# An encoder layer on one NeuronCore: more pairs of seven products in the up projection, and edits around its beginning and around the down projection

## The chip, the core and the metric

The kernel runs on one core of a Trainium2 chip. A core has TensorE (PE in the profile; PEld is its weight load), VectorE (DVE), ScalarE (ACT), GpSimd (POOL) and SyncE (SP); SBUF is the working memory of 128 partitions, PSUM the eight accumulator banks of TensorE, and DRAM the memory off the core. The metric is the device time of one execution in microseconds (us); less is better.

## The reference

One layer of an encoder: 256 tokens, width 2048, all in float32. The first half has two attention branches, a gate for each and an output projection. Its second half, which the change touches, is a squared-ReLU MLP between two RMS norms with a residual sum:

```python
y = jnp.einsum('bsd,de->bse', mixed, w_out[l])
x = x + rms_norm(y, norm_mix_post[l])
h = rms_norm(x, norm_mlp_pre[l])
u = jnp.square(jax.nn.relu(jnp.einsum('bsd,df->bsf', h, w_up[l])))
x = x + rms_norm(jnp.einsum('bsf,fd->bsd', u, w_down[l]), norm_mlp_post[l])
```

`w_up` is 2048 x 8192 and `w_down` 8192 x 2048: the up and the down projection each read 64 MB of weights and take half of the matmul work between them.

## The kernel before, in words

**Products in three matmuls.** Each float32 operand is split into a high and a low part (ACT casts the high part, DVE subtracts it to get the low part), and each product is three matmuls: high times high, high times low, low times high (`Products.add`, L642 to 653). All their records stand at L649.

**Pairs by eight or by seven.** Weights come in tiles of 256 rows by 1024 columns, called a pair here (two blocks of 128 rows); `pair_weights` (L602) loads one on SP's queue and splits it. With the 256 tokens as two blocks of 128, a pair is a 2 x 2 by 2 x 2 block product. `eight` forms it in the plain way: for each of four output pieces two products, 24 matmuls. `seven` uses Strassen's scheme in Winograd's form: seven products, 21 matmuls. For that the weights' sums are formed too (L614 to 616, L626, L627 on DVE and ACT; names with `t`, `eh`, `el`) and the activations' sums (`sums_of`, L714).

**Banks.** The plain pieces accumulate in products 1, 2, 3 and 7, in the four banks of the pool `mm`. Products 0, 4, 5 and 6, which only pairs of seven use, lie in the four banks of the pool `ms` from the first pair of seven of a group to its last, when `combine` (L673) adds them up on DVE. The transposes through PSUM (`bank(name)`) use `ms` too.

**Up projection (L1025 to 1057).** Eight groups of 1024 columns, each `wide_group` (L682) over eight pairs. Group 0 runs all pairs by eight; groups 1 to 7 run `UPS`, pairs 3 and 5 by seven. The gate groups earlier in the kernel run `MIXED` (L749), pairs 0, 3 and 6 by seven. At each pair a hook (`up_each`) emits side work: in group 0 the rest of the residual rows and their transposes (`residual_parts`, L865; results `h2T`), the squares for the norm (`mlp_squares`) and the sums for the pairs of seven (`h2sum`); in the others the transposes, squares (L1012) and splits of what the group before gave, half a group at pair 1 and half at pair 2 (`u_sets`, L1001, and `act_sets`, L944). These are written to DRAM on POOL's queue (`keeph`, `keepl`).

**Before the up projection.** The last group of the output projection is finished row block by row block; `between` (L896) emits the first two `residual_parts` of rows 0 to 127 between its products. `post_norm` gives the scale `ry` of a row block through a power on POOL (L86 to 89).

**Down projection (L1100 to 1143).** Two halves `g` of 1024 output columns. Each runs blocks of four pairs; the activations come back from DRAM on ACT's queue (`act_again`, L976; names `bh`, `bl`). In most blocks two of the four pairs go by seven, in the first and in the last block of each half one. In the last block `in_order` chains the matmuls in program order; the last pair's four pieces go one by one to DVE and ACT (`down_piece`, L1078), and `finish` (L1087) forms the norm of a row block, adds the residual `x2` and writes the rows out.

**Buffers and order.** SBUF tiles of 4 KB a partition come from a pool of 27 pages; weights have three buffers each for the raw tile, the high and the low part, the sums' parts five. The order of instructions on each engine is fixed ahead by a planner that goes by program order and by a timeline with estimated durations; `issue_after` lets an instruction come behind a given one on its engine. Each engine works its list in that order.

Of the kernel before, what the change touches and what calls it, by code (L numbers as in the profile page):

```python
# [38 lines left out]
def encoder_layer(ctx: ExitStack, tc: tile.TileContext, a, out):  # L39
# [42 lines left out]
    def inv_rms(ss, n, name, r=None):  # L82

        w = ss.shape[1]
        ms_ = small(w, f"{name}_m")
        nc.vector.tensor_scalar(ms_, ss, 1.0 / n, EPS, op0=ALU.mult, op1=ALU.add)  # L86
        if r is None:
            r = small(w, f"{name}_r")
        nc.gpsimd.tensor_tensor(r, ms_, expo[:, :w], op=ALU.pow)
        return r  # L90


    last_load = [None]

# [507 lines left out]
    def pair_weights(view, name, seven, low=None):  # L602


        raw = wp.tile([P, 4, 512], F32, tag="raw", name=f"{name}r")
        last_load[0] = nc.sync.dma_start(raw.rearrange("p (h b) c -> p h (b c)", h=2), view).ins
        h1, l1 = wtile("hi", f"{name}h"), wtile("lo", f"{name}l")
        if not seven:
            nc.scalar.copy(h1, raw)  # L609
            nc.vector.tensor_sub(l1, raw, h1.bitcast(F32))  # L610
# [3 lines left out]
        nc.vector.tensor_add(t[0], raw[:, 1:3], raw[:, 0:1].to_broadcast([P, 2, 512]))  # L614
        nc.vector.tensor_add(t[1][:, 0], t[0][:, 0], raw[:, 2])
        nc.vector.tensor_add(t[1][:, 1], t[1][:, 0], raw[:, 3])
        nc.vector.tensor_sub(l1[:, 1:4], raw[:, 1:4], h1[:, 1:4].bitcast(F32))
        h2, l2 = [], []
        for i in range(2):
            for part, n in ((h2, "eh"), (l2, "el")):  # L620
                shape, n = [P, 2, 512], f"{name}{n}{i}"
                if low and part is l2:
                    part.append(low(shape, F32R, n))
                else:
                    part.append(mid.tile(shape, F32R, tag="e", name=n))
            nc.scalar.copy(h2[i], t[i])  # L626
            nc.vector.tensor_sub(l2[i], t[i], h2[i].bitcast(F32))  # L627
        return h1, l1, h2, l2
# [3 lines left out]
    class Products:  # L632
# [22 lines left out]
        def seven(self, stat, w, last):  # L655
# [3 lines left out]
            self.add(0, stat(0), r, 1, last)  # L659
            self.add(2, stat(6), r, 2)  # L660
            self.add(1, stat(1), r, 3)
            self.add(4, stat(3), t[0], 0, last)
# [19 lines left out]
    def wide_group(name, kinds, view, stat7, stat8, mm_banks, z, piece, each=None, turn=None):  # L682
# [5 lines left out]
        for n, (i, seven) in enumerate(kinds):  # L688
            if each:
                each(n)  # L690
            w = pair_weights(view(i), f"{name}_{i}", seven)
# [203 lines left out]

    def between(i):  # L896
        return residual_parts(0, i - 5)[0] if i in (5, 6) else None
# [27 lines left out]

    def first_up(n):
# [12 lines left out]
    kept = {}  # L939
# [85 lines left out]
    UPS = [(0, 0), (1, 0), (2, 0), (3, 1), (4, 0), (5, 1), (6, 0), (7, 0)]  # L1025
    uz = None
    for g in range(DFF // 1024):
        z = [page([P, 2, 512], F32, f"u{g}{t}") for t in range(2)]

        def up_each(n, g=g, uz=uz):  # L1030
            if not g:
                first_up(n)
                if n == 7:
                    for i in (3, 5):
# [5 lines left out]
            elif n in (1, 2):  # L1040
                u_sets(g * 2 - 3 + n, uz)
# [3 lines left out]
            UPS if g else ALL8,  # L1045
# [9 lines left out]
            turn=None if g else partial(residual_parts, 1, 0),  # L1055
# [31 lines left out]
    def finish(t):  # L1087
# [3 lines left out]
        for c in range(4):  # L1091
# [3 lines left out]
                z, z, rd, x2[t * 2 + c // 2][:, cs], op0=ALU.mult, op1=ALU.add  # L1095
# [5 lines left out]
    for g in range(2):  # L1101
        pr = Products(f"p{g}", (1, 2, 3, 7))
        for bi, b in enumerate(blocks[g]):
            end = bi == len(blocks[g]) - 1
            if bi == 0:
                steps = [(b + 1, 0, 0), (b, 1, 0), (b, 0, 1), (b + 1, 1, 0)]
# [5 lines left out]
            for n, (cg, j, seven) in enumerate(steps):  # L1112
# [9 lines left out]
                if g == 1 and bi == 5 and n == 0:  # L1122
                    gp2 = [page([P, 1024], F32, f"gp2{h}") for h in range(2)]
                    for h in range(2):
# [3 lines left out]
                        )  # L1128
                if g == 1 and bi == 6:
# [69 lines left out]
```

## Time and profile before

| | |
|---|---|
| three runs | 1367.77, 1370.4, 1371.29 us (median 1370.4) |
| profiled execution, its own time | 1367.94 us |
| its span, first to last instruction | 1366.2 us |
| granted TensorE clock, mean | 0.997 |
| busy: PE, PEld, DVE, ACT, POOL | 98%, 82%, 76%, 53%, 2% |
| moved between DRAM and SBUF | 329.57 MB, 241 GB/s |
| up projection, first to last product | about 659 to 1016 us of the span |
| down projection | about 1017 us to the end |

Times in the rows are microseconds from the start of the span. A row of a timeline gives start, length, engine, line, operation, output<-inputs with partitions x elements, and in brackets how long the engine had been idle and what ended it. Durations of neighbouring rows on one engine can overlap, so the price of an operation in a row of them is the distance from start to start.

### The profile page before, as it was taken

The page shows a single profiled execution, that of the slowest core. Times are in us where ns is not written, and L with a number is a line of the kernel's source. Part 1 is how long each engine was busy: PE and PEld are TensorE (multiplying, and loading weights), DVE is VectorE, ACT ScalarE, POOL GpSimd, SP SyncE. Part 2 cuts the span into 40 slices and gives each one's busy share as a digit, 9 for nine tenths or more (in the row PEclk, how much of TensorE's full clock was granted, in tenths as well). Part 3 has the DMA queues.
Part 4 walks back from the last instruction along what each step waited for, and adds up shares of the span by engine and source line. Part 5 has one row for each costly group of instructions (what it writes and reads, how often), then busy time and mean ns, then how long its engine had stood idle before and what let it go on. Part 6 is the DMA issues. An engine that isn't in the chain of part 4 may idle for free.

```text
span 1366.2 us, 16268 instructions
## 1 busy us (share of the span) xinstructions
PE 1340.7 (98%) x6347; PEld 1119.4 (82%) x6347; DVE 1034.7 (76%) x1181; ACT 717.8 (53%) x843; POOL 33.9 (2%) x67
## 2 busy tenths in 40 slices
PE   7999999999999999999999999999999999999996
PEld 6888888888888888888788888888887788888885
DVE  6878866667857886654768887888788888798886
ACT  7455455555644464344465655666555555454542
POOL 0000000000000000000000000000000000000000
PEclk9999999999999999999999999999999999999998
DMA  8675645564556655676367766786697999698891
GB/s 306 201 227 168 202 161 175 166 206 154 185 185 213 218 185 185 204 264 205 134 207 260 259 244 243 258 287 231 249 336 282 386 355 373 239 385 346 340 352 74
DMA packets 115245, 329.57 MB, mean 241 GB/s; under 512 B 17120, under 2 KB 18400, under 8 KB 115168
## 3 DMA queue, kind: packets, MB, share of 16 engines
q1 hardware_dynamic: 96784, 264.03, 56.1%
q10 hardware_dynamic: 12240, 40.91, 7.7%
q0 software_dynamic: 6144, 23.60, 4.3%
q8 instruction: 50, 0.82, 0.2%
q14 instruction: 27, 0.22, 0.0%
HBM read 302.81 MB, written 27.51 MB: 242 GB/s over the span
## 4 chain that ended last, share of the span: by engine, by line
PE 96%; DVE 1%; DMA 1%; issue 0%; ACT 0%; ACTq 0%; SPq 0%; DVEq 0%; POOLq 0%; POOL 0%
PE u L649 25%; PE p L649 23%; PE ga L649 6%; PE gb L649 6%; PE ba L649 3%; PE bb L649 3%; PE qa_p L192 2%; PE ka_p L192 2%; PE qn_p L192 2%; PE kn_p L192 2%; PE y_p L230 2%; PE y_p L231 2%; PE y_p L232 2%; PE qa_p L193 1%; PE qn_p L193 1%; PE kn_p L193 1%
## 5 line engine op out<-in xcount | busy, mean ns | idle before, releaser
L117 DVE TENSOR_TENSOR y_l<-y_w,y_h 128x1024 fp32r<-128x1024 f32 x32 | 37.9, 1222 | 30.9 <-ACT y_h L116 30.9
L116 ACT CAST y_h<-y_w 128x1024 fp32r<-128x1024 f32 x32 | 32.0, 1047 | 40.9 <-PE y_p L232 32.6
L230 PE MATMUL y_p<-y_h,mh 128*128 128x512 f32 x128 | 50.1, 391 | 0.0
L231 PE MATMUL y_p<-y_l,mh 128*128 128x512 f32 x128 | 49.9, 390 | 0.0
L232 PE MATMUL y_p<-y_h,ml 128*128 128x512 f32 x128 | 49.8, 390 | 0.0
L192 PE MATMUL qa_p<-hT,qa_h 128*128 128x512 f32 x128 | 47.1, 413 | 1.2 <-DVE hT L275 1.2
L649 PE MATMUL u<-u_0h,h2T 128*128 128x512 f32 x128 | 44.6, 392 | 2.3 <-DVE ry_m L86 1.1
L192 PE MATMUL qn_p<-hT,qn_h 128*128 128x512 f32 x128 | 45.9, 400 | 0.0
L192 PE MATMUL kn_p<-hT,kn_h 128*128 128x512 f32 x128 | 45.4, 398 | 0.0
L192 PE MATMUL ka_p<-hT,ka_h 128*128 128x512 f32 x128 | 45.0, 398 | 0.0
L649 PE MATMUL u<-u_1h,h2T 128*128 128x512 f32 x128 | 44.6, 396 | 0.0
L649 PE MATMUL u<-u_4h,h2T 128*128 128x512 f32 x128 | 42.1, 390 | 0.0
L649 PE MATMUL u<-u_2h,h2T 128*128 128x512 f32 x128 | 41.8, 397 | 0.0
L649 PE MATMUL u<-u_6h,h2T 128*128 128x512 f32 x128 | 41.8, 389 | 0.0
L649 PE MATMUL u<-u_7h,h2T 128*128 128x512 f32 x128 | 41.0, 389 | 0.0
L193 PE MATMUL qn_p<-hT,qn_l 128*128 128x256 f32 x128 | 35.9, 281 | 0.0
L193 PE MATMUL kn_p<-hT,kn_l 128*128 128x256 f32 x128 | 35.7, 280 | 0.0
L193 PE MATMUL qa_p<-hT,qa_l 128*128 128x256 f32 x128 | 35.2, 285 | 0.0
L193 PE MATMUL ka_p<-hT,ka_l 128*128 128x256 f32 x128 | 35.2, 280 | 0.0
L609 ACT CAST u_1h<-u_1r 128x2048 fp32r<-128x2048 f32 x8 | 15.3, 1913 | 36.1 <-PE u L649 32.6
L649 PEld LDWEIGHTS u<-u_0h,h2T 128*128 128x128 f32 x128 | 23.9, 188 | 8.4 <-DVE ry_m L86 1.6
L192 PEld LDWEIGHTS qa_p<-hT,qa_h 128*128 128x128 f32 x128 | 24.6, 194 | 6.7 <-DVE hT L275 1.6
(1386 smaller groups left out, 4346.8 us busy)
## 6 DMA issues: line engine op xcount, KB each, us to landing
y_w<-in_w_out SPq DMA_DIRECT2D x16, 1024.0 KB, 5.3
bh<-keeph ACTq DMA_DIRECT2D x30, 512.0 KB, 9.2
bl<-keepl ACTq DMA_DIRECT2D x30, 512.0 KB, 11.1
keeph<-ah POOLq DMA_DIRECT2D x18, 512.0 KB, 3.4
keepl<-al POOLq DMA_DIRECT2D x18, 512.0 KB, 7.2
ka_w<-in_w_in SPq DMA_DIRECT2D x8, 1024.0 KB, 5.7
va_w<-in_w_in SPq DMA_DIRECT2D x8, 1024.0 KB, 5.0
qn_w<-in_w_in SPq DMA_DIRECT2D x8, 1024.0 KB, 5.1
```

The lines of the kernel that those rows point to most:

```text
L116: nc.scalar.copy(hi[part], raw[part])
L117: nc.vector.tensor_sub(lo[part], raw[part], hi[part].bitcast(F32))
L192: nc.tensor.matmul(ps[b], hi[:, k % 4, cs], mv, start=(k == 0), stop=False)
L193: nc.tensor.matmul(ps[b][:, :T], lo[:, k % 4, cs], mv[:, :T], start=False, stop=(k == nk - 1))
L230: nc.tensor.matmul(ps[t], sh, hi[:, k % 4], start=(k == 0), stop=False)
L231: nc.tensor.matmul(ps[t], sh, lo[:, k % 4], start=False, stop=False)
L232: nc.tensor.matmul(ps[t], sl, hi[:, k % 4], start=False, stop=(k == nk - 1))
L609: nc.scalar.copy(h1, raw)
L649: ins = nc.tensor.matmul(self.ps[i], st, mv[:, blk], start=i not in self.begun, stop=last and n == 2).ins
```

## The change

In the up projection, groups 1 to 7 run the order `MIXED` and so have three pairs by seven, one of them (pair 0) second in the group; `h2sum` is formed for pairs 0, 3 and 6; both `u_sets` are emitted at pair 1; and `seven` issues its products in the order 2, 1, 0, 4, 6, 5, 3. In group 0, two subtractions of weights (`u_1l` and `u_2l`) get a place on DVE: `u_1l` behind the last DVE instruction (a low half of `h2T`) of the second of the two `residual_parts` in `between`, `u_2l` behind the scaling in the last `inv_rms`, which is that of `post_norm` for rows 128 to 255. After the squares of group 0 the four pages of `x2` are written to DRAM, and they are loaded again as `x3` at the first pair of the last block, on ACT's queue. In the down projection the first block of the first half has no pair by seven, and in the very last block the last two pairs are worked together, piece by piece.

```diff
 def inv_rms:
-        nc.vector.tensor_scalar(ms_, ss, 1.0 / n, EPS, op0=ALU.mult, op1=ALU.add)
+        scaled[0] = nc.vector.tensor_scalar(
+            ms_, ss, 1.0 / n, EPS, op0=ALU.mult, op1=ALU.add
+        ).ins
...
-    def pair_weights(view, name, seven, low=None):
+    def pair_weights(view, name, seven, low=None, after=None):
...
             nc.scalar.copy(h1, raw)
-            nc.vector.tensor_sub(l1, raw, h1.bitcast(F32))
+            with tc.issue_after(after) if after else nullcontext():
+                nc.vector.tensor_sub(l1, raw, h1.bitcast(F32))
...
-            self.add(0, stat(0), r, 1, last)
             self.add(2, stat(6), r, 2)
             self.add(1, stat(1), r, 3)
+            self.add(0, stat(0), r, 1, last)
...
+    tail = []
+
     def between(i):
-        return residual_parts(0, i - 5)[0] if i in (5, 6) else None
+        if i in (5, 6):
+            last, act, vec = residual_parts(0, i - 5)
+            tail.append((act, vec))
+            return last
...
     def first_up(n):
         for t, c in {2: [(1, 1), (0, 2)], 3: [(1, 2), (0, 3)], 4: [(1, 3)]}.get(n, ()):
             residual_parts(t, c)
+        if n == 1:
+            return tail[1][1]
+        if n == 2:
+            return scaled[0]
         if n == 5:
             for t in range(2):
                 mlp_squares(t)
                 mlp_scale(t)
+            for i in range(4):
+                kd = dram.tile([P, 1024], F32, name=f"keepx{i}", tag=f"keepx{i}")
+                nc.gpsimd.dma_start(kd, x2[i])
+                kept["x", i] = kd
...
-    UPS = [(0, 0), (1, 0), (2, 0), (3, 1), (4, 0), (5, 1), (6, 0), (7, 0)]
...
             if not g:
-                first_up(n)
+                after = first_up(n)
                 if n == 7:
-                    for i in (3, 5):
+                    for i in (0, 3, 6):
...
-            elif n in (1, 2):
-                u_sets(g * 2 - 3 + n, uz)
+                return after
+            elif n == 1:
+                for q in (2, 1):
+                    u_sets(g * 2 - q, uz)
...
-            UPS if g else ALL8,
+            MIXED if g else ALL8,
...
             z = zw[c // 2, t][:, c % 2]
             nc.vector.scalar_tensor_tensor(
-                z, z, rd, x2[t * 2 + c // 2][:, cs], op0=ALU.mult, op1=ALU.add
+                z, z, rd, x3[t * 2 + c // 2][:, cs], op0=ALU.mult, op1=ALU.add
             )
...
             if bi == 0:
-                steps = [(b + 1, 0, 0), (b, 1, 0), (b, 0, 1), (b + 1, 1, 0)]
+                steps = [(b + 1, 0, 0), (b, 1, 0), (b, 0, g), (b + 1, 1, 0)]
...
+                if end and g and n == 0:
+                    x3 = [page([P, 1024], F32, f"x3{i}") for i in range(4)]
+                    for i in range(4):
+                        nc.scalar.dma_start(x3[i], kept["x", i])
...
                 last = end and n == 3
+                if g and end and n > 1:
+                    ahead = [*ahead, (cg, j, w)] if last else [(cg, j, w)]
+                    if not last:
+                        continue
+                else:
+                    ahead = [(cg, j, w)]
                 for which in range(4):
-                    pr.eight(partial(dstat8, sets[g, cg], cg, j), w, which, last)
+                    for m, (cc, jj, ww) in enumerate(ahead):
+                        pr.eight(
+                            partial(dstat8, sets[g, cc], cc, jj), ww, which, last and m == len(ahead) - 1
+                        )
```

More of the change, by code (lines that the diff above doesn't have):

```diff
@@ L93, in encoder_layer @@
     last_load = [None]
+    scaled = [None]
     def load(src, k0, nk, c0, cw, name):
@@ L688, in wide_group @@
         for n, (i, seven) in enumerate(kinds):
-            if each:
-                each(n)
-            w = pair_weights(view(i), f"{name}_{i}", seven)
+            after = each(n) if each else None
+            w = pair_weights(view(i), f"{name}_{i}", seven, after=after)
             if seven:
@@ L894, in residual_parts, with turn_rows @@
         return last.ins, act.ins, vec.ins
+    tail = []
     def between(i):
-        return residual_parts(0, i - 5)[0] if i in (5, 6) else None
+        if i in (5, 6):
+            last, act, vec = residual_parts(0, i - 5)
+            tail.append((act, vec))
+            return last
+    def turn_rows():
+        residual_parts(1, 0)
     def mlp_squares(t):
@@ L924, in encoder_layer @@
         )
+    kept = {}
     def first_up(n):
@@ L932, in first_up @@
                 mlp_scale(t)
+            for i in range(4):
+                kd = dram.tile([P, 1024], F32, name=f"keepx{i}", tag=f"keepx{i}")
+                nc.gpsimd.dma_start(kd, x2[i])
+                kept["x", i] = kd
     NG = DFF // 512
     FIRST = (NG - 4, NG - 2)
-    kept = {}
     def seven_of(cg):
@@ L1054, in encoder_layer @@
             each=up_each,
-            turn=None if g else partial(residual_parts, 1, 0),
+            turn=None if g else turn_rows,
         )
```

## The prediction

> **What bounds the kernel now.** I read the page's busy times and the chain of waits first, then busy times by stretch, then each engine's timeline in the stretches that the change touches.
>
> ```profile
> PE 1340.7 (98%) x6347; PEld 1119.4 (82%) x6347; DVE 1034.7 (76%) x1181; ACT 717.8 (53%) x843; POOL 33.9 (2%) x67
> PE 96%; DVE 1%; DMA 1%; issue 0%; ACT 0%; ACTq 0%; SPq 0%; DVEq 0%; POOLq 0%; POOL 0%
> ```
>
> TensorE (PE) is the chain. So there are three ways to win: fewer products, fewer of the few gaps on PE, and a shorter stretch behind its last product. By stretch (start:end, length, then PE, PEld, DVE, ACT, POOL busy, granted clock, DMA share, GB/s):
>
> ```profile
> 440.80:482.30 41.50, 41.50 (x185) 34.37 (x184) 36.26 (x34) 22.08 (x17) 0.00 (x0) 1.00 0.59 203
> 640.00:664.00 24.00, 21.77 (x98) 16.97 (x96) 14.94 (x22) 11.07 (x17) 0.55 (x1) 1.00 0.51 173
> 664.00:711.00 47.00, 46.92 (x219) 39.00 (x220) 30.80 (x59) 30.17 (x54) 1.67 (x3) 1.00 0.52 176
> 843.00:887.00 44.00, 44.00 (x204) 36.47 (x203) 35.85 (x35) 25.99 (x26) 3.22 (x6) 1.00 0.74 257
> 1019.00:1063.00 44.00, 41.53 (x182) 31.75 (x180) 34.39 (x31) 25.92 (x26) 3.19 (x6) 1.00 0.79 299
> 1063.00:1107.00 44.00, 42.89 (x188) 35.19 (x189) 40.87 (x35) 23.45 (x19) 0.00 (x0) 1.00 0.95 364
> ```
>
> The first row is a gate group in the order MIXED (three pairs of seven), the fourth an up group with two: PE has no gap in either. The gaps are 2.2 us where the up projection begins (second row) and 2.5 + 1.1 = 3.6 us where the down projection begins (the last two). The clock is 1.00, so a product saved is worth its full-speed time.
>
> **Price of a product.** From the chain of waits (start, length, what):
>
> ```profile
> 802.80 0.77 PE uT L1009 x7
> 846.91 0.77 PE uT L1009 x7
> 853.30 37.67 PE u L649 x166
> ```
>
> 166 products in 37.67 us are 0.227 us each; one up group lasts 846.91 - 802.80 = 44.1 us. A pair by eight products is 24 matmuls (each product is hi-hi, hi-lo, lo-hi), by seven 21: it saves 3 x 0.227 = 0.68 us. The Trainium skill ("TensorE: Matmul & The Clock Gate", Back-to-back issue gap) gives about 131 ns for a sustained 512-column matmul; by it seven more pairs would save 2.8 us. The rows above disagree at 227 ns, and the measurement decides.
>
> **Part 1, up groups 1 to 7.** Three pairs of seven for two: 7 x 0.68 = **-4.8 us** on PE, if VectorE (DVE) keeps up. Its price for the two kinds of pair, start to start in its timeline:
>
> ```profile
> 842.11 2.29 DVE L610 TENSOR_TENSOR u_1l<-u_1r,u_1h 128x2048 fp32r<-128x2048 f32 x1
> 844.31 2.28 DVE L610 TENSOR_TENSOR u_2l<-u_2r,u_2h 128x2048 fp32r<-128x2048 f32 x1
> 859.43 1.22 DVE L614 TENSOR_TENSOR u_3t<-u_3r 128x1024 f32<-128x1024 f32 x1
> 860.57 1.75 DVE L617 TENSOR_TENSOR u_5l<-u_5r,u_5h 128x1536 fp32r<-128x1536 f32 x1
> 862.23 0.69 DVE L615 TENSOR_TENSOR u_3t<-u_3t,u_3r 128x512 f32<-128x512 f32 x1
> 862.84 1.22 DVE L614 TENSOR_TENSOR u_5t<-u_5r 128x1024 f32<-128x1024 f32 x1
> 863.97 1.22 DVE L627 TENSOR_TENSOR u_3el<-u_3t,u_3eh 128x1024 fp32r<-128x1024 f32 x1
> ```
>
> A plain pair takes 2.20 us of DVE. A pair of seven takes L614 1.14, L617 1.66, L615 and L616 (the same size) 0.6 each, and twice L627, as long as L614, 1.14: 6.3 us. So a group's DVE time goes from 35.85 to about 39.9 us, while the group shrinks from 44.1 to 43.4: 92% full. The cover for the extra 4.1 us is DVE's idle time, 8.1 us a group now. Does it bend? The gate group above has the same order of pairs and 36.3 us in 41.5 (87%) with PE full, and 1063 to 1107 has 93% while DVE was catching up. I take most of it as covered: bounds 0 and 0.7 us a group (0.7 would eat the saving), taken 0.1, **+0.7 us** in all. ScalarE (ACT) gets about 1.6 us more (casts below: three quarters of 1.91 and twice 1.05, for one of 1.91) on 26 of 44 and does not bind. The third set of sums in group 0 is 1536 elements of DVE work, less than a plain pair, beside 30.8 of 47 us busy (row 664 to 711): nothing, but up to 1 us if that cover is gone, since pair 0 is now second in group 1.
>
> Moved with it: both transposed sets of the group before (u_sets) now come at pair 1. They issue 16 transposes, four squares on ACT, 12 copies and subtractions and six POOL DMAs. The transposes use the four small PSUM banks, which pair 0 needs too, at once:
>
> ```profile
> 852.81 0.49 PE L1009 MATMUL uT<-ident,u 128*128 128x128 f32 x3
> 855.77 1.07 ACT L1012 ACTIVATE u<-uT 128x512 f32<-128x512 f32 x2
> 858.62 0.39 PE L649 MATMUL u<-u_3h,h2T 128*128 128x512 f32 x1
> ```
>
> Today the last square ends (856.84) 3.9 us after the last transposes began, and the next pair of seven starts only at 858.62. After the change PE has six matmuls of pair 0 (1.4 us, products 2 and 1 now come first) and the plain pair behind it (5.4 us) to fill that time, so I take 0; bounds 0 and 3.9 - 1.4 = 2.5 us a group (the slower rival).
>
> **Part 2, x2 to DRAM and back.** Four writes on POOL's queue after the squares of group 0, behind the two powers, 0.53 us of issue each like the rows counted in POOL's 3.22 us for six; nothing on POOL is due until group 1. It frees four pages of 27 (one goes to the third set of sums). At the end four loads of 512 KB wait on ACT's queue for free pages; behind them stand ACT's casts of pairs d1120, d1121 and d1131, and PE waits for these.
>
> ```profile
> 1324.00:1330.00 6.00, 6.00 (x29) 4.95 (x28) 4.45 (x4) 2.81 (x2) 0.00 (x0) 1.00 1.02 409
> 1336.00:1342.00 6.00, 6.00 (x28) 4.95 (x27) 3.99 (x3) 2.43 (x3) 0.00 (x0) 1.00 0.00 0
> 1338.62 1.91 ACT L609 CAST d1131h<-d1131r 128x2048 fp32r<-128x2048 f32 x1 [2.58 <-issue]
> 1340.56 2.29 DVE L610 TENSOR_TENSOR d1131l<-d1131r,d1131h 128x2048 fp32r<-128x2048 f32 x1 [2.01 <-ACT d1131h L609]
> 1343.13 0.39 PE L649 MATMUL p<-d1121h,bh 128*128 128x512 f32 x1
> ```
>
> 2.1 MB at 409 GB/s are 5.1 us, in a stretch where the DMA engines are full; from 1336 on they are empty. So d1131r, the last weight, lies ready 2.6 us before its cast, and its low half 1.6 us before it will be wanted (1343.13 + 1.4, part 5, against 1342.85): 5.1 us later costs 0.9. If a pair before it has only the 1.6, it costs 3.5. Bounds 0 and 3.5 us, taken **+0.4**, as not all of the 5.1 us need fall on weights.
>
> **Part 3, where the up projection begins.**
>
> ```profile
> 657.54 2.29 DVE L610 TENSOR_TENSOR u_1l<-u_1r,u_1h 128x2048 fp32r<-128x2048 f32 x1
> 659.74 1.12 DVE L886 SCALAR_TENSOR_TENSOR h2T<-h2T_t,g_mlp,h2T 128x128 fp32r<-128x128 f32 x4
> 661.33 1.14 ACT L885 ACTIVATE h2T<-h2T_t,g_mlp 128x128 fp32r<-128x128 f32 x4
> 664.08 0.72 PE L649 MATMUL u<-u_0h,h2T 128*128 128x512 f32 x2 [1.12 <-DVE ry_m L86]
> 664.87 0.40 PE L649 MATMUL u<-u_1l,h2T 128*128 128x512 f32 x1
> ```
>
> u_1l and u_2l stand on DVE before the halves of h2T that PE waits for. u_1l is put behind the last of those halves, u_2l behind ry_m. What is late next: u_1l itself, which PE reads at 664.87, 0.8 us behind the gap. If ACT keeps its order (h2T to 662.47, the row at 661.33), DVE's four halves end about 662.8 and u_1l's 2.2 us at 665.0: nothing is won. If ACT too does h2T first, ahead of the cast u_2h that now stands in front of it and is as long as d1131h's 1.91, all of it comes 2 us sooner. So the gain lies between -2.2 (all of the gap) and 0; I take **-1.0**, half way.
>
> **Part 4, where the down projection begins.** The first block loses its pair of seven: PE **+0.7**, DVE -4.1, ACT -1.6 (the prices of part 1).
>
> ```profile
> PE p L649 <- DMA bh<-keeph: 1.6, 3, 0.9
> PE p L649 <- ACT d001eh L626: 0.8, 2, 0.6
> PE p L649 <- DVE d011l L610: 0.6, 1, 0.6
> 1052.51 1.05 ACT L626 CAST d000eh<-d000t 128x1024 fp32r<-128x1024 f32 x1 [3.75 <-DVE d000t L616]
> ```
>
> These waits are 3.0 us of the 3.6. The DMAs among them stand on ACT behind the cast of the last row, which waited 3.75 us for DVE; 4.1 us less on DVE and three more pages move both forward. Bounds -3.6 and 0, taken **-2.5**.
>
> **Part 5, last pairs by piece.** All matmuls stay; the four pieces now end 2.7 us apart, not 1.4.
>
> ```profile
> 1353.79 0.39 PE L649 MATMUL p<-d1131h,bl 128*128 128x512 f32 x1
> 1355.47 0.18 ACT L1083 ACTIVATION_READ_ACCUMULATOR jd<-zw 128x1 f32 x1
> 1356.37 2.73 DVE L1094 SCALAR_TENSOR_TENSOR zw<-zw,rd_r,x 128x512 f32<-128x512 f32 x4
> 1359.31 0.54 POOL L89 TENSOR_TENSOR rd_r<-rd_m,expo 128x1 f32<-128x1 f32 x1 [3.09 <-DVE rd_m L86]
> 1359.88 2.74 DVE L1094 SCALAR_TENSOR_TENSOR zw<-zw,rd_r,x 128x512 f32<-128x512 f32 x4 [0.72 <-POOL rd_r L89]
> ```
>
> Today rows 0 to 127 are scaled (2.73 us) between the last square and the power for rows 128 to 255. With their piece done 5.4 us before PE's end they are out of that path: square read at 1355.65, sum and scale 0.35, power and its signal 0.85, so the last four start at about 1356.9, not 1359.88: **-3.0** (bounds -3.6, and 0 if their place on DVE stays).
>
> **Sum.** -4.8 + 0.7 + 0.4 - 1.0 + 0.7 - 2.5 - 3.0 = **-9.5 us**, against the profiled execution's own 1367.94 (span 1366.2): 1358.4. The median of the runs shown is 1370.4, which gives 1360.9; the three runs spread over both, and I name 1359.5 between them. 0.3%, about what a measurement of this kernel can tell from no change, is 4.1 us.
>
> **Rivals.** (a) *Slower: the small banks.* The squares stay behind casts on ACT as today, and PE stands at pair 0's third product, 2.5 us in each of seven groups: +17.5, so 1377. It decides from 1.9 us a group on, where the 9.5 us and 4.1 more are gone. For it: the row at 855.77; against it: PE has the plain pair to go on with. Chance 0.12. (b) *DVE becomes the bound.* If half of its 8.1 us idle cannot be used, a group is 39.9 + 4.1 = 44.0 us, and part 1 gives nothing: +4.1 on the forecast, 1363.5. For it: 92%; against: the gate group. Chance 0.18. (c) *The openings don't do what they say*: u_1l and the DMAs from DRAM are the next waits, the gaps of parts 3 and 4 stay, +1.0 + 2.5, so 1363; with (b) 1367. For it: u_1l's 0.8 us. Chance 0.10. The forecast: 0.60, with its own range of 1355 to 1364.
>
> Faster by over 0.3% are the forecast and most of (b) and (c): 0.76; within 0.3% is what is left of those: 0.12; slower 0.12. The range of 1354 to 1370 leaves out (a) and little else; its lower end is every gain in full (-4.8 - 2.2 - 3.6 + 0.7 - 3.6 = -13.5 on 1367.9).
>
> **What would show it.** 6329 matmuls on PE (21 fewer, 3 more). An up group of 43.4 us, with DVE at about 40 and no wait of PE: right; 44 with DVE over 41: (b); a PE gap in front of pair 0's products with ACT's L1012 as releaser: (a). PE full from 1019 on: part 4. About 9 us, not 12, from PE's last matmul to the end: part 5. The forecast is wrong if up groups grow, or if the loads at the end hold PE over 2 us.

## The result, and the profile after

The kernel after takes 1420.33 us (median of four runs, 1418.69 to 1421.75) against 1369.37 us before in the same comparison: the ratio is 1.0376, interval 1.0357 to 1.0395. It is 51 us slower; the forecast was 1359.5 us, and no rival came near. The profiled execution took 1421.67 us, its span is 1419.9 us, its mean granted clock 0.985.

First the busy times and the chain of waits of the page after, then the largest waits of PE from the up projection on (what was waited for; us in total, times, longest):

```profile
PE 1356.5 (96%) x6329; PEld 1126.2 (79%) x6329; DVE 1062.4 (75%) x1218; ACT 727.2 (51%) x856; POOL 38.2 (3%) x71
PE 86%; DMA 4%; DVE 3%; ACT 3%; issue 3%; SPq 0%; DVEq 0%; POOLq 0%; ACTq 0%
```

```profile
PE u L653 <- ACT u_6h L617: 24.6, 7, 5.4
PE u L653 <- DVE u_4l L614: 9.5, 7, 1.4
PE u L653 <- ACT u_4h L612: 5.9, 7, 1.0
PE p L653 <- DVE d1131l L614: 2.8, 1, 2.8
PE u L653 <- DVE ry_m L86: 0.8, 1, 0.8
```

The matmuls are the 6329 foreseen, and PE's chain now has DMA, DVE and ACT in it. The three first waits come seven times each, once in every changed up group: 40.0 us, 5.7 a group. They wait for weights (`u_4`, `u_6`), not for the sums, and none waits for a square of u_sets. Where the down projection begins there is no wait left, and where the up projection begins 0.8 us.

Four landmarks show where the time went: the first product of the up projection, the first of the down projection, the end of the last matmul, and the end of the span.

| us | before | after | difference |
|---|---|---|---|
| to the first up product | 658.76 | 659.53 | +0.8 |
| up projection | 357.88 | 412.91 | +55.0 |
| down projection to the last matmul's end | 337.54 | 336.58 | -1.0 |
| behind it | 12.02 | 10.88 | -1.1 |
| span | 1366.2 | 1419.9 | +53.7 |

Two up groups after, and the stretch from 1060 us with most of the down projection (columns as in the prediction):

```profile
786.00:838.00 52.00, 46.77 (x202) 37.66 (x201) 39.66 (x39) 26.94 (x27) 3.24 (x6) 0.95 0.63 216
838.00:890.00 52.00, 47.04 (x206) 37.93 (x205) 41.25 (x42) 28.11 (x29) 3.24 (x6) 0.97 0.63 219
1060.00:1368.00 308.00, 308.00 (x1368) 255.10 (x1367) 260.41 (x218) 160.31 (x131) 3.19 (x6) 1.00 0.89 341
```

A group that was to shrink from 44.1 to 43.4 us lasts about 52. DVE has the 40 us of work that were forecast, but in 52 us it is 76 to 79% busy: it isn't full. PE is idle 5 us a group, and the clock is 0.95 to 0.97, which is some 2 us more of each 52.

One group from three sides: DVE's timeline, the loads of the raw weight tiles on SP's queue, and the chain of waits.

```profile
862.59 2.29 DVE L614 TENSOR_TENSOR u_2l<-u_2r,u_2h 128x2048 fp32r<-128x2048 f32 x1
869.61 1.76 DVE L621 TENSOR_TENSOR u_3l<-u_3r,u_3h 128x1536 fp32r<-128x1536 f32 x1 [4.73 <-ACT u_3h L617]
876.69 2.29 DVE L614 TENSOR_TENSOR u_4l<-u_4r,u_4h 128x2048 fp32r<-128x2048 f32 x1 [0.58 <-ACT u_4h L612]
878.90 1.22 DVE L988 TENSOR_TENSOR al<-u,ah 128x1024 fp32r<-128x1024 f32 x1
880.04 1.22 DVE L618 TENSOR_TENSOR u_0t<-u_0r 128x1024 f32<-128x1024 f32 x1
883.03 0.69 DVE L620 TENSOR_TENSOR u_0t<-u_0t,u_0r 128x512 f32<-128x512 f32 x1
889.04 0.69 DVE L620 TENSOR_TENSOR u_3t<-u_3t,u_3r 128x512 f32<-128x512 f32 x1
```

```profile
852.50 0.37 SPq L609 DMA_DIRECT2D u_3r<-in_w_up  x1
864.90 0.37 SPq L609 DMA_DIRECT2D u_4r<-in_w_up  x1
879.01 0.37 SPq L609 DMA_DIRECT2D u_6r<-in_w_up  x1
883.75 0.37 SPq L609 DMA_DIRECT2D u_5r<-in_w_up  x1
889.75 0.37 SPq L609 DMA_DIRECT2D u_7r<-in_w_up  x1
```

```profile
876.69 2.30 DVE u_4l L614
879.01 6.77 DMA u_6r<-in_w_up
885.86 1.48 ACT u_6h L617
887.38 26.82 PE u L653 x117
```

The sums of `u_0` and `u_3` begin at 880.04, directly behind the last split of u_sets (878.90, `al`). Until their last sum is formed (883.7 and 889.7) the raw tiles of both stay occupied. Of three raw buffers one is left to turn: `u_2` gives it free at 864.88, `u_4` is asked for at 864.90; `u_4` gives it free at 878.98, `u_6` is asked for at 879.01. The two tiles let go by the sums are taken at 883.75 and 889.75. So `u_6` comes 6.77 us of load and 1.48 us of cast behind `u_4`, and PE waits: in its list two of the 12 matmuls of `u_0` that need sums stand ahead of `u_6`'s first (884.15 and 887.38), the other ten of `u_0` and all 12 of `u_3` behind it.

The buffers of the high parts are all taken there too. The cast `u_3h` starts at 868.10, behind 4.50 us in which ACT was idle; the last matmul that reads `u_1h`, three high parts earlier, ends at 868.02 (867.63, 0.39 long). Before, the same cast starts at 846.76 and the last matmul on `u_0h` ends at 846.68. No run changes the number of these buffers, so their share of the loss isn't known.

How long a raw tile is held, from its load's issue to the end of the last instruction that reads it (worked out from the timelines, median over the groups; the last two kernels are experiments below):

| held, us | pairs of seven | sum of all eight | sum / 3 |
|---|---|---|---|
| before | u_3 30.0, u_5 24.9 | 131.6 | 43.9 |
| after | u_0 38.1, u_3 37.4, u_6 14.3 | 156.4 | 52.1 |
| two pairs of seven at places 3 and 5 | u_3 29.7, u_6 22.9 | 131.5 | 43.8 |
| two at places 1 and 3 | u_0 33.9, u_3 34.6 | 157.7 | 52.6 |

A third of the sum is the length of the group in each to within 1 us, as it must be when three buffers are always taken (with other choices of groups the sums move by up to 3 us). The table says where the time sits, not what causes what; that took the experiments.

### The profile page after: what moved, and what is told of

Same layout as the page of the kernel before. It is cut to its first block, busy times and chain, and to the rows that moved or that the text cites. A ratio compares the mean times of both kernels' runs of the same rounds, so it can differ in the third digit from the quotient of the medians.

```text
span 1419.9 us, 16296 instructions
## 1 busy us (share of the span) xinstructions
PE 1356.5 (96%) x6329; PEld 1126.2 (79%) x6329; DVE 1062.4 (75%) x1218; ACT 727.2 (51%) x856; POOL 38.2 (3%) x71
## 4 chain that ended last, share of the span: by engine, by line
PE 86%; DMA 4%; DVE 3%; ACT 3%; issue 3%; SPq 0%; DVEq 0%; POOLq 0%; ACTq 0%
PE p L653 23%; PE u L653 17%; PE ga L653 6%; PE gb L653 6%; DMA u_6r<-in_w_up 4%; PE ba L653 3%; PE bb L653 3%; PE qa_p L195 2%; PE ka_p L195 2%; PE qn_p L195 2%; PE kn_p L195 2%; PE y_p L234 2%; PE y_p L233 2%; PE y_p L235 2%; DVE u_4l L614 1%
## 5 line engine op out<-in xcount | busy, mean ns | idle before, releaser
L653 PE MATMUL u<-u_4h,h2T 128*128 128x512 f32 x128 | 46.7, 426 | 5.9 <-ACT u_4h L612 5.9
L653 PE MATMUL u<-u_5h,h2T 128*128 128x512 f32 x128 | 41.9, 389 | 0.0
L653 PE MATMUL u<-u_4l,h2T 128*128 128x512 f32 x64 | 27.9, 436 | 9.5 <-DVE u_4l L614 9.5
L653 PEld LDWEIGHTS u<-u_4h,h2T 128*128 128x128 f32 x128 | 25.5, 204 | 13.9 <-ACT u_4h L612 8.9
L621 DVE TENSOR_TENSOR u_3l<-u_3r,u_3h 128x1536 fp32r<-128x1536 f32 x7 | 12.3, 1758 | 31.5 <-ACT u_3h L617 31.5
L617 ACT CAST u_0h<-u_0r 128x1536 fp32r<-128x1536 f32 x7 | 10.4, 1486 | 48.5 <-PE u L653 48.3
```

Source lines behind the costliest of these rows:

```text
L653: ins = nc.tensor.matmul(self.ps[i], st, mv[:, blk], start=i not in self.begun, stop=last and n == 2).ins
```

## Experiments

Theory A, formed after the result: the sums of pairs of seven asked for behind u_sets stand on DVE behind its splits, raw tiles are held for it, and weights come late. B: DVE has too much work (the prediction's rival b). C: the small banks (its rival a). All times are medians; "before" lay between 1368.2 and 1368.8 in these comparisons. Where one edit needs several places, the main one is shown and `...` marks a cut.

**Which part loses.** Everything of the change but its up groups: order, sums and u_sets there as before.

```diff
-                    for i in (0, 3, 6):
+                    for i in (3, 5):
...
-            elif n == 1:
-                for q in (2, 1):
-                    u_sets(g * 2 - q, uz)
+            elif n in (1, 2):
+                u_sets(g * 2 - 3 + n, uz)
...
-            MIXED if g else ALL8,
+            [(0, 0), (1, 0), (2, 0), (3, 1), (4, 0), (5, 1), (6, 0), (7, 0)] if g else ALL8,
```

> The changed kernel with the up groups 1 to 7 as before (order UPS, sums of pairs 3 and 5, u_sets at pairs 1 and 2); all the other parts of the change stay. All theories: the loss is in the up groups, so it goes. The rest was forecast at -5 us against before; the trace after shows no gap where the down projection begins and a wait of 2.8 us near the end: 1360 to 1366 us. If the loss came from x2's way through DRAM or from the edits at the beginning, this stays above 1400.

1363.82 us, ratio 0.9968 (0.9954 to 0.9981). Its stretches:

```profile
843.00:887.00 44.00, 44.00 (x204) 36.46 (x203) 35.86 (x35) 26.17 (x25) 3.22 (x6) 1.00 0.73 257
1019.00:1063.00 44.00, 44.00 (x204) 36.52 (x203) 36.52 (x34) 25.29 (x26) 3.18 (x6) 1.00 0.96 358
```

The whole loss, 56.5 us, is in the up groups; the rest of the change gains 0.3%.

**The sums ahead of u_sets.** Pair 0's weights asked for ahead of u_sets, and in a second kernel those of places 1, 2 and 3.

```diff
+            early = seven and n == 1
+            if early:
+                w = pair_weights(view(i), f"{name}_{i}", seven)
             after = each(n) if each else None
-            w = pair_weights(view(i), f"{name}_{i}", seven, after=after)
+            if not early:
+                w = pair_weights(view(i), f"{name}_{i}", seven, after=after)
```

> The changed kernel, but pair 0's weights are asked for before the transposed sets (u_sets) and no longer behind them. Theory A (pages: the sums u_0t get their two pages only when u_sets is done with its nine; till then pair 0's and pair 3's raw tiles are held, one raw buffer of three is left for the rest, and PE waits for u_4 and u_6): u_0t moves ahead of u_sets' splits, one more raw buffer turns over, and most of the 5.7 us of PE waits per up group go: 1360 to 1385 us. Theory B (DVE is the bound at 92%): the work is the same, so 1410 to 1425 us. Theory C (the four small PSUM banks): pair 0's banks are still asked for behind the transposes, 1410 to 1425 us.

```diff
+            if not n:
+                held = {}
+            if any7 and each and n == 1 and kinds[1][1]:
+                for m in (1, 2, 3):
+                    held[m] = pair_weights(view(kinds[m][0]), f"{name}_{kinds[m][0]}", kinds[m][1])
             after = each(n) if each else None
-            w = pair_weights(view(i), f"{name}_{i}", seven, after=after)
+            w = held.get(n) or pair_weights(view(i), f"{name}_{i}", seven, after=after)
```

> The changed kernel with the weights of places 1, 2 and 3 (pairs 0, 2 and 3) asked for ahead of u_sets, so that the sums of pairs 0 and 3 get their pages first. With only pair 0 ahead it was 1390.4 us against 1420. If the sums' late pages are the cause, the sums of pair 3 also come in DVE's idle time in front of u_sets and the time falls further, to 1360 to 1380 us. If their lateness is a symptom (PE, ACT and DVE wait for one another through the three hi/lo buffers), 1388 us or more.

1390.40 us (1.0164, 1.0148 to 1.0179) and 1381.07 us (1.0085, 1.0070 to 1.0100): 30 and 39 us less with the same work on every engine, each a little above the range that theory A had named. So B falls as the cause of these. What PE waits for in the second:

```profile
PE u L653 <- DVE u L1047: 6.6, 5, 1.4
PE u L653 <- DVE u_0l L621: 6.2, 5, 1.3
```

The waits for `u_4` and `u_6` are gone; two smaller ones, where a group ends, stand in their place.

**A fourth raw buffer**, and two pages fewer.

```diff
-    pages = ctx.enter_context(tc.tile_pool(name="pages", bufs=27))
+    pages = ctx.enter_context(tc.tile_pool(name="pages", bufs=25))
...
-        raw = wp.tile([P, 4, 512], F32, tag="raw", name=f"{name}r")
+        raw = wp.tile([P, 4, 512], F32, tag="raw", bufs=4, name=f"{name}r")
```

> The changed kernel with four raw weight buffers and 25 pages (the room does not hold 27). Theory A: the sums stay late in DVE's order, but two raw buffers are left beside the two held ones, u_6r is issued some 10 us sooner, and the wait on u_6h (24.6 us in all) mostly goes: 1385 to 1400 us. Theories B and C: the number of raw buffers does not matter, 1415 to 1430 us (two pages fewer do no good).

1396.15 us (1.0206, 1.0189 to 1.0223): 24 us less, of which 21 are in the up projection (391.6 for 412.9 us); the down projection is 4.8 us shorter, with no wait for `d1131l` left in it. PE's wait for `u_6h` falls from 24.6 to 9.5 us. The raw tiles do carry much of the delay; the sums stay late.

**Place or number.** Two pairs of seven at places 1 and 3, two at places 3 and 5 (both u_sets at place 1 in either), and three at places 3, 5 and 6 (u_sets at 1 and 2 as before). The activations' sums (`h2sum`) follow the pairs; only the order is shown.

```diff
-            MIXED if g else ALL8,
+            [(1, 0), (0, 1), (2, 0), (3, 1), (4, 0), (6, 0), (5, 0), (7, 0)] if g else ALL8,
```

> The changed kernel with two pairs by seven only, pairs 0 and 3 at places 1 and 3, both u_sets at place 1 (pair 6 plain). Theory P: pair 0 still stands second beside u_sets, 1380 to 1410 us. Theory N: two pairs fit, 1362 to 1370 us.

```diff
+            [(1, 0), (0, 0), (2, 0), (3, 1), (4, 0), (6, 1), (5, 0), (7, 0)] if g else ALL8,
```

> The changed kernel with two pairs by seven at the usual places 3 and 5 (pairs 3 and 6; pair 0 plain), but both u_sets at place 1. Theories P and N: as fast as with the up groups as before, 1362 to 1368 us. If it is the two u_sets together at place 1 that costs (transposes and splits in one go), 1380 us or more.

```diff
+            [(1, 0), (2, 0), (4, 0), (0, 1), (5, 0), (3, 1), (6, 1), (7, 0)] if g else ALL8,
```

> The changed kernel with three pairs by seven in each up group, but at places 3, 5 and 6 (order 1, 2, 4, 0, 5, 3, 6, 7; counted from 0) and u_sets half at place 1 and half at place 2, as before. Theory P (place: a pair of seven second in the group, beside both u_sets, is what goes wrong): the waits go, 1357 to 1364 us. Theory N (number: with three pairs by seven the sums come too late wherever they stand, since they wait for the pages of u_sets): 1380 to 1420 us.

1424.91 us (1.0406, 1.0389 to 1.0422), 1364.09 us (0.9966, 0.9955 to 0.9978) and 1410.36 us (1.0298, 1.0278 to 1.0318). Two pairs of seven, as before, lose as much as three when they stand at places 1 and 3, and nothing at 3 and 5. The largest waits of the first:

```profile
PE u L653 <- ACT u_6h L612: 12.4, 7, 1.8
PE u L653 <- DVE u_0el L631: 12.0, 7, 1.7
```

With places 3 and 5 both u_sets at one pair cost nothing (1364.09 against 1363.82). That alone doesn't test C, which needs a pair of seven beside them. C falls by the waits, since in none of these kernels does PE wait for a square of u_sets, and by the kernel with pair 0's weights first, where the banks are asked for behind the transposes as in the kernel after and 30 us go. But place isn't all: three from place 3 on lose 46 us. Its largest wait is for the last additions of the group before (`u` at L1042, 13.5 us), one that also stands in the kernels whose sums come early; the raw tiles of its first two pairs of seven are held 34 and 32 us.

**Early sums by other buffers.** The tiles of the sums get two, then four buffers of their own instead of pages.

```diff
-    pages = ctx.enter_context(tc.tile_pool(name="pages", bufs=27))
+    pages = ctx.enter_context(tc.tile_pool(name="pages", bufs=25))
...
-        t = [page([P, 2, 512], F32, f"{name}t{i}") for i in range(2)]
+        t = [wp.tile([P, 2, 512], F32, tag="tt", name=f"{name}t{i}", bufs=2) for i in range(2)]
```

> The changed kernel with the sums of weights (t) in two buffers of their own, and 25 pages instead of 27: the same room. Theory A: the sums no longer wait for pages, u_0t and u_3t move ahead of u_sets' splits, both raw tiles are released early, PE's waits on u_4 and u_6 go: 1355 to 1372 us. Theories B and C: 1410 to 1425 us.

(four: `bufs=4` there, and 23 pages)

> The changed kernel with the sums of weights in four buffers of their own and 23 pages. With two such buffers and 25 pages it was 1414.8 us: the sums did come early, but the two buffers were then the shortage. Theory A2: with four, the sums of pairs 0 and 3 come in front of u_sets and do not wait for one another, 1360 to 1390 us. If it is the number of pages that matters (A1), 23 for the rest are too few, 1420 us or more.

1414.80 us (1.0351, 1.0321 to 1.0381) and 1416.10 us (1.0348, 1.0329 to 1.0367): both misses. The sums did come ahead of u_sets, and in all next to nothing was won. With four, in the profiled execution, the up projection took 402.7 us, 10 less than in the kernel after, and the down projection, with four pages fewer, 343.5, 7 more. PE waits 21.3 us for `u_2l` and 7.9 for the `u` additions, and every raw tile but two is held 19 to 23 us. In one of its groups DVE forms `u_0t` and `u_0el` (851.90 to 859.65) ahead of the split `u_2l` (864.76). The cast `u_3h` comes at 874.77, again 0.08 us behind the last matmul on `u_1h`. Early sums alone aren't the cure; why these two orders lose as much as the first isn't settled.

**Pages.** The kernel after without the trip of x2 through DRAM, so that four pages fewer are free.

```diff
-                kd = dram.tile([P, 1024], F32, name=f"keepx{i}", tag=f"keepx{i}")
-                nc.gpsimd.dma_start(kd, x2[i])
-                kept["x", i] = kd
...
-                    x3 = [page([P, 1024], F32, f"x3{i}") for i in range(4)]
-                    for i in range(4):
-                        nc.scalar.dma_start(x3[i], kept["x", i])
...
-                z, z, rd, x3[t * 2 + c // 2][:, cs], op0=ALU.mult, op1=ALU.add
+                z, z, rd, x2[t * 2 + c // 2][:, cs], op0=ALU.mult, op1=ALU.add
```

> The changed kernel with x2 left in its four pages (no writes to DRAM, no loads at the end); everything else stays, three pairs by seven and both u_sets at place 1 too. Theory A1 (shortage: the sums of pair 0 wait until enough of the 27 pages are free): four pages fewer make it worse, 1428 to 1450 us. Theory A2 (turn: pages are handed out in the order in which the program asks for them, so the sums asked for behind u_sets cannot overtake its last tile, however many are free): the sums stand at the same place in DVE's order, and the time is that of the changed kernel, 1414 to 1424 us.

1414.56 us (1.0327, 1.0307 to 1.0346). With four pages fewer the sums stand at the same place and a group lasts no longer, which speaks against a shortage of pages as what makes them late, the reason that the first expectations had named.

**What is left with three pairs' weights ahead** (1381.07 us, 17 more than with the up groups of before). First a fourth raw buffer there too, then the sums of the up groups on POOL.

> The kernel with the weights of places 1, 2 and 3 asked for ahead of both u_sets (1381.07 us), and now four raw buffers instead of three, two pages fewer (25). It computes everything. Still open there are 17 us against the kernel with the up groups of before (1363.8); its up group takes 46.6 us, and its PE waits are DVE's u adds (6.6 us) and u_0l (6.2 us), both where a group ends. Theory R, raw tiles are still too few (the holds of a group sum to 139.9 us over three buffers): the fourth takes the rest away, 1359 to 1367. Theory D, DVE is bunched where a group ends (relu adds, combine, the sums and splits of u_0 and u_3 one behind the other): a buffer more changes no order on DVE, 1377 to 1385, the same two waits.

```diff
+        add = (nc.gpsimd if name[0] == 'u' else nc.vector).tensor_add
-        nc.vector.tensor_add(t[0], raw[:, 1:3], raw[:, 0:1].to_broadcast([P, 2, 512]))
+        add(t[0], raw[:, 1:3], raw[:, 0:1].to_broadcast([P, 2, 512]))
...
```

> The kernel with the weights of places 1, 2 and 3 asked for ahead of both u_sets (1381.07 us), and in the up groups the three additions that make t of a pair of seven are done by POOL instead of DVE. It computes everything. DVE has 2.6 us less to do for each pair, 7.8 us a group, most of it where a group ends. Theory D (DVE is bunched there): the waits for u_0l and for the u adds go, 1360 to 1368. Theory R (raw tiles): a raw tile is held until POOL has read it, so it hangs on POOL's own duration; with POOL as fast as DVE 1372 to 1382. Theory P, POOL takes over twice as long as DVE for these additions (the trace has only its additions on 128x2, 0.55 to 0.77 us), holds the tiles longer and keeps its own DMA issues waiting: over 1385.

1378.90 us (1.0078, 1.0063 to 1.0093) and 1381.21 us (1.0092, 1.0074 to 1.0109). The first kernel keeps both waits (8.0 and 6.7 us): raw tiles aren't what is left. The second tells little on DVE's load, because DVE got slower. Groups of DVE's instructions between 700 and 1080 us, with the sums on POOL and then with them on DVE:

```profile
L632 DVE TENSOR_TENSOR u_0el<-u_0t,u_0eh 128x1024 fp32r<-128x1024 f32 x14 | 34.3, 2451 | 0.0
L614 DVE TENSOR_TENSOR u_2l<-u_2r,u_2h 128x2048 fp32r<-128x2048 f32 x7 | 22.0, 3138 | 1.8 <-ACT u_2h L612 1.8
```

```profile
L631 DVE TENSOR_TENSOR u_0el<-u_0t,u_0eh 128x1024 fp32r<-128x1024 f32 x14 | 16.9, 1216 | 0.0
L614 DVE TENSOR_TENSOR u_2l<-u_2r,u_2h 128x2048 fp32r<-128x2048 f32 x7 | 16.0, 2280 | 0.0
```

In that stretch DVE was busy 339.0 us with 252 instructions, against 322.6 us with 314: the fewer took longer.

**Order where a group ends**, still with three pairs' weights ahead. The sums put behind the last addition of the group before; then the same with x2 kept in its pages; then the split `u_2l` behind that addition too.

```diff
-            nc.vector.tensor_add(zt, zt, ps)
+            added[0] = nc.vector.tensor_add(zt, zt, ps).ins
...
-        nc.vector.tensor_add(t[0], raw[:, 1:3], raw[:, 0:1].to_broadcast([P, 2, 512]))
+        with tc.issue_after(added[0]) if added[0] and name[0] == "u" else nullcontext():
+            nc.vector.tensor_add(t[0], raw[:, 1:3], raw[:, 0:1].to_broadcast([P, 2, 512]))
...
```

> The kernel with the weights of places 1, 2 and 3 asked for ahead of both u_sets (1381.07 us), with one thing more: in the up groups the additions that make t stand on DVE behind the last addition that ends the group before (the u adds ahead of the relu). It computes everything; no buffer, load or amount of work changes. In the kernel without it PE waits 1.3 us for u_0l and 1.4 us for the last u adds in each group, and u_0t, u_0t and u_3t (0.68 to 1.22 us each) stand ahead of these on DVE. Theory D' (these sums in that place are the rest): both waits fall under 0.5 us, 1358 to 1368. Theory S (21 pairs of seven leave DVE no room anywhere in the group, the wait only moves): 1375 to 1385, with other waits, behind u_0el or the splits of u_sets.

> The same as the kernel with the sums behind the last u adds, and x2 stays in its pages instead of the trip through DRAM. Where both hold, D' and that the trip costs some 4 us (1363.8 against 1360.0 with the up groups of before): 1354 to 1362, the 4.8 us that seven pairs of seven more save then show against 1360.0. By S: 1370 to 1381.

```diff
-                    held[m] = pair_weights(view(kinds[m][0]), f"{name}_{kinds[m][0]}", kinds[m][1])
+                    held[m] = pair_weights(view(kinds[m][0]), f"{name}_{kinds[m][0]}", kinds[m][1], after=added[0])
```

> The kernel with the sums behind the last u adds and x2 in its pages (1373.3 us), and the split u_2l of the plain pair at place 2 behind the last u adds as well. It computes everything. There PE waited 7.3 us for u_2l in three of the seven groups and 3.3 us for the u adds; in each of these DVE did u_2l (2.28 us) between two of the u adds, in the others PE lost nothing. Theory D', DVE's order where a group ends: these waits go in most groups, 1357 to 1366. Theory S, DVE has no room left and the wait only moves: 1369 to 1377, the same total of waits on u_0l, u_3l or u_0el.

1376.53 us (1.0052, 1.0036 to 1.0068), 1373.30 us (1.0032, 1.0022 to 1.0042) and 1373.83 us (1.0031, 1.0017 to 1.0046). The first step gains 4.5 us. In the second kernel the waits that are left stand in three groups of seven (first fence); the third takes that wait away and gets others in its place (second fence; its last row is a square of u_sets, C's wait, 1.4 us in all):

```profile
PE u L655 <- DVE u_2l L615: 7.3, 3, 2.4
PE u L655 <- DVE u L1045: 3.3, 3, 1.1
```

```profile
PE u L655 <- DVE u L1045: 9.6, 10, 1.1
PE u L655 <- ACT u_5h L613: 1.6, 3, 0.8
PE u L655 <- ACT u L1035: 1.4, 3, 0.5
```

Of the two theories for the rest the one by which the wait only moves held (theory S). It doesn't show that three pairs of seven can't be had: in the second kernel PE had no gap from 740 to 780 us with DVE busy 36.2 of 40. Some groups run full, others don't. What separates them, and whether an order exists in which all do, stays open. Putting u_sets behind the first pair of seven wasn't tried, since its transposes need banks that a group's pairs of seven hold until `combine`.

**The other parts alone.** Up groups as before and x2 kept in its pages; and, on the first kernel of this section, the pair of seven put back into the first block of the down projection.

> The changed kernel with the up groups as before (this alone: 1363.8 us) and x2 left in its pages. The wait of 2.8 us on d1131l near the end comes from DVE's order: the four additions of combine stand ahead of d1131l, since the loads of x3 shift the plan. Without them d1131l stands ahead: 1360 to 1362.5 us. If the four pages are what closes the gap where the down projection begins, that gap of 3.6 us is back and the time is 1363 to 1366 us.

```diff
-                steps = [(b + 1, 0, 0), (b, 1, 0), (b, 0, g), (b + 1, 1, 0)]
+                steps = [(b + 1, 0, 0), (b, 1, 0), (b, 0, 1), (b + 1, 1, 0)]
```

> The changed kernel with the up groups as before (this alone: 1363.8 us) and with the pair by seven put back into the first block of the down projection. If the plain pair is what closes the gap there (DVE and ACT late), the 3.6 us come back less 0.7 us of PE: 1366 to 1367 us. If the freed pages are, 1363 us or less.

1359.97 us (0.9935, 0.9921 to 0.9949) and 1370.95 us (1.0012, 1.0003 to 1.0022). The first is the fastest kernel of this study, faster than both kernels: the change without its up groups and without the trip of x2. The second gives back 7.1 us, more than the 2 to 3 that were expected: the waits for `bh`, `bl`, `d000eh` and `d011l` where the down projection begins are back (2.8 us), so the plain first block is what closes the gap there.

## Why the prediction was wrong, point by point

**Part 1 (-4.8 + 0.7) failed, and by the sentence "I take most of it as covered".** The up projection came out 55.0 us longer, 57.0 if its beginning's gain of 2.0 (below) is taken off. The counted work was right: 6329 matmuls, 40 us of DVE a group. What failed is the cover. I judged it by DVE's idle share of a group and by the gate groups, which run the same order of pairs but have no u_sets. An idle share doesn't say when in the group an instruction's turn comes. In the up groups the sums of two pairs came behind u_sets' splits, their raw tiles were held 37 to 38 us, and one buffer of three was left to turn. Shown: moving the sums ahead takes away 39 us, a fourth raw buffer 21 in the up projection, and two pairs of seven at places 1 and 3 lose as much without any added work. Not settled: the other 13 to 17 us, the two misses, three pairs from place 3 on, and the part of the buffers for high and low parts. The named waits are 40.0 us of the loss. The clock adds to it: with PE idle in pieces it was 0.95 to 0.97 over the groups, some 2 us in each.

**The small banks (rival a)**, priced at nothing with an upper end of 2.5 us a group: nothing was right, since in the kernel after PE never waits for the squares of u_sets. The rival forecast the right sign by a mechanism that isn't there. **Rival (b)** named DVE, at 0.6 us a group; the loss was 8, and not by DVE being full.

**Part 2 (+0.4, upper end 3.5):** 1363.82 against 1359.97 us, +3.9, just over the upper end. It isn't the loads. The "1.6 us" of slack of `d1131l` were read from an order that the change itself moved: its cast now stands on ACT behind the copy of `combine`, and itself behind `combine`'s four additions. DVE and PE with the up groups of before and x2 through DRAM:

```profile
1334.66 0.69 DVE L681 TENSOR_TENSOR zw<-zw,p 128x512 f32<-128x512 f32 x1 [4.19 <-PE p L653]
1336.72 0.68 DVE L684 TENSOR_TENSOR zw<-p,zw 128x512 f32<-128x512 f32 x1
1337.31 2.28 DVE L614 TENSOR_TENSOR d1131l<-d1131r,d1131h 128x2048 fp32r<-128x2048 f32 x1
```

```profile
1339.65 0.50 PE L653 MATMUL p<-d1131l,bh 128*128 128x512 f32 x1 [2.83 <-DVE d1131l L614]
```

Without the trip `d1131l` starts at 1333.97, ahead of the four, and PE doesn't wait.

**Part 3 (-1.0, from -2.2 to 0): the mechanism right, the size near the range's end.** The gap fell from 2.2 to 0.8 us, and the up projection with its groups as before is 2.0 us shorter (355.89 for 357.88). The condition held: ACT took the last `h2T` (659.04) ahead of the cast `u_2h` (659.29). The next thing late is `u_1l`, as written: it ends at 662.38, and PE goes on at 662.44 (the row names `ry_m`, which came behind it on DVE).

```profile
660.10 2.28 DVE L614 TENSOR_TENSOR u_1l<-u_1r,u_1h 128x2048 fp32r<-128x2048 f32 x1
662.44 0.50 PE L653 MATMUL u<-u_1l,h2T 128*128 128x512 f32 x1 [0.84 <-DVE ry_m L86]
```

**Part 4 (+0.7 - 2.5): right in sign, too small.** In the fastest kernel the down projection is 4.6 us shorter (332.93 for 337.54), against -1.8, and beyond its lower end of -2.9. The lower end of -3.6 was the idle time; the price of the gap was larger, as a count of matmuls shows. Before, then the fastest kernel:

```profile
1048.00:1056.00 8.00, 7.35 (x30) 5.46 (x31) 6.85 (x7) 2.31 (x3) 0.00 (x0) 1.00 0.74 265
1056.00:1064.00 8.00, 5.96 (x20) 2.98 (x18) 5.75 (x5) 4.79 (x4) 0.00 (x0) 1.00 1.03 411
```

```profile
1048.00:1056.00 8.00, 8.00 (x37) 6.63 (x36) 8.00 (x8) 3.16 (x3) 0.00 (x0) 1.00 1.03 409
1056.00:1064.00 8.00, 8.00 (x37) 6.64 (x36) 4.44 (x5) 3.84 (x3) 0.00 (x0) 1.00 1.02 391
```

PE was idle 2.7 of these 16 us, but 24 matmuls are missing, 24 x 0.227 = 5.4 us: the second row counts 20 matmuls as 5.96 us busy, 0.30 us each, at a clock of 1.00. The pages freed by x2 have little part in it: the fastest kernel doesn't free them and has 0.5 us of gap left there.

**Part 5 (-3.0): mis-sized, -1.4** (12.02 to 10.62 us in the fastest kernel). I had the last four scalings start 2.7 us behind PE's end; it is 4.3. The rows are those with the up groups of before (matmul's end 1350.83, scaling 1355.14); the fastest kernel has the same 4.3 (1347.58, 1351.90).

```profile
1348.75 2.74 DVE L1114 SCALAR_TENSOR_TENSOR zw<-zw,rd_r,x 128x512 f32<-128x512 f32 x4
1352.00 0.69 DVE L1100 TENSOR_TENSOR zw<-zw,p 128x512 f32<-128x512 f32 x1
1355.14 2.74 DVE L1114 SCALAR_TENSOR_TENSOR zw<-zw,rd_r,x 128x512 f32<-128x512 f32 x4 [0.72 <-POOL rd_r L91]
```

The scaling of rows 0 to 127 left the path, and stood in the way of the last piece instead: its addition (1352.00) comes 1.2 us behind the last matmul because DVE was still at it and at the instruction behind it. And the product of that piece with `gp` (1353.48) stands ahead of its sum (1354.09) on DVE, 0.6 us that the prediction had left out.

Parts 3, 4 and 5 together were put at -5.8 us and gave -8.0 in the fastest kernel.

## What to carry to other kernels

Price an edit of order by what is held while an instruction waits for its turn, not by an engine's idle share: list each buffer from its load to its last reader, and see how many are left to turn. Judge cover by a stretch that has the same side work, not by one with the same main loop. And undo parts one at a time: the change had 8 us of gain in it, hidden under the up groups, which lost 57, and the trip of x2, which lost 3.9.

## What the runs showed of the hardware

**The clock halved behind a gap of 2.83 us.** Behind PE's wait for `d1131l` (it goes on at 1339.65), in the kernel with the up groups of before:

```profile
1340.00:1342.00 2.00, 2.00 (x8) 1.58 (x7) 0.69 (x1) 0.03 (x1) 0.00 (x0) 0.70 0.04 8
1342.00:1344.00 2.00, 2.00 (x7) 1.54 (x6) 0.69 (x1) 0.69 (x2) 0.00 (x0) 0.50 0.00 0
1344.00:1346.00 2.00, 2.00 (x10) 1.69 (x9) 0.57 (x1) 0.00 (x0) 0.00 (x0) 0.95 0.00 0
```

```profile
1341.00 0.63 PE L653 MATMUL p<-d1121h,bh 128*128 128x512 f32 x1
1341.43 0.63 PE L653 MATMUL p<-d1121l,bh 128*128 128x512 f32 x1
```

From 1341.00 to 1343.99 matmuls start 0.43 us apart instead of 0.227: seven times 0.2, some 1.4 us lost on top of the 2.83, with PE busy all the while. The length of a gap alone doesn't decide it. In the kernel with the pair of seven put back into the first block PE waits 3.2 us for `d1131l`, and the clock behind it stays at 1.00. In the kernel after, two gaps of 0.99 and 1.36 us in one group are followed by 0.57 (828 to 832 us), the same two in the group before it by 1.00 (775 to 779 us). The Trainium skill ("TensorE: Matmul & The Clock Gate", What's actually happening) says that the gate goes to half rate after an idle window of about 3.4 us; the half rate agrees, but here a shorter gap was enough, and the halving came 1.3 us after PE had gone on.

**POOL's additions slow DVE's.** With the sums on POOL those of 128x512 took means of 2.2 to 3.3 us there (0.69 on DVE), and DVE's instructions beside them took up to twice their time (2451 for 1216 ns above). The split `u_7l`, which had none of POOL's additions beside it, kept its 2.28 us. The Trainium skill ("Perfetto Trace Analysis", Optimizing Scalar/DVE Operations) warns that the two share a port to SBUF, so that moving work between them might not help; these rows and the time (1381.21 for 1381.07 us) agree, though no row shows the port itself.
